# A hybrid decoder layer on one core: block one's softmax ahead of block two's masks, block two's transposes over four PSUM banks, the keys' transposes after both rotations

## The chip, the core and the metric

The kernel runs on one core of a Trainium2 chip. The metric is the device time of one execution in microseconds; lower is better. TensorE (PE) multiplies matrices, VectorE (DVE) and ScalarE (ACT) do the elementwise work, and SyncE (SP) issues the loads of the weights.

## The reference

One decoder layer over 256 tokens (two blocks of 128) of width 2048, in float32. Cut to what matters here:

```
h = rmsnorm(x); proj = h @ w_in
xr, yr, q, k, v, g_rnn, g_attn = split(proj)
xr = rg_lru(causal_conv(xr));  y_rnn = xr * gelu(yr)
q, k = rope(q), rope(k)                       # 32 query heads, 4 key/value heads of 64
scores = q k^T * 64**-0.5, masked: at most 127 tokens back, causal
m = max(max(scores), sink); p = exp(scores - m)
probs = p / (sum(p) + exp(sink - m));  y_att = probs @ v
mix = sigmoid(g_rnn) * (y_rnn @ w_rnn_proj) + sigmoid(g_attn) * (y_att @ w_attn_proj)
x = x + rmsnorm(mix @ w_out)
x = x + rmsnorm(relu(rmsnorm(x) @ w_mlp_up)**2 @ w_mlp_down)
```

## The kernel before

Every weight is streamed once from HBM in halves of 128 x 1024 float32. ScalarE rounds a half to its high part (`whi`, L94), VectorE subtracts to get the low part (`wlo`, L95), and TensorE makes three products of high and low parts for each tile. The `Stream` object splits about six halves ahead of their use, in six buffers for each part, and loads into four more (`wraw`).

The stages follow one another: keys and values; then for each of four groups of heads (one key/value head and eight query heads, `g` = 0 to 3) a pass over the attention's gates (`g`, 96 matmuls with 512 columns, two accumulators in one pair of PSUM banks, ended by `tanh` on ScalarE, L647) and a pass over the queries (`q`, 96 matmuls); then the recurrence's projections (`recur`, in calls of `a_pair`), the projections of the mixers, the output projection, and the MLP.

The work that belongs to no weight pass is written as generators in a list `waiting`. A pass calls `pump()` at fixed places, which runs the first generator to its next `yield`. `keys_values` runs in the first gates' pass. `attention(g)` begins after the queries' pass of group g and so runs in the next group's two passes, and for the last group in the four `a_pair` calls of `recur(0)`. A scheduler orders each engine's instructions from there; those that `pin` marks keep their order. Each engine then works through its own list strictly in order, and waits where a semaphore is not there yet.

`first_norm` (L434) gets the rows' norms, scales the rotation's tables, and spreads the norm over the partitions by two matmuls (`pr`, L448), copied by ScalarE to `rT` (L449), which `conv` and `gelu` use much later. `keys_values` (L515) rotates a block's keys, has them transposed by TensorE (`pk`, L526) and copied to `kT` (L527), and then does the second block.

In `attention` (L532), the queries are rotated and transposed (`pq`). `scores(tb, j, banks)` multiplies them with the keys (`sc`, L560), and VectorE scales and masks the scores (L566) and takes their maximum (L568). `softmax(tb)` makes the small statistics on VectorE (L575 to L577), the exponentials with their sums on ScalarE (L582), and normalises on VectorE (L584, L585, L587). `turn_probs(tb)` transposes the probabilities on TensorE (`pt`, L604), eight transposes for block one and sixteen for block two, four to a bank, and ScalarE copies each bank (L606). The output matmuls (`po`, L630) follow. Block one sees 128 keys, block two 256, so block two's scores take twice as many passes.

PSUM has eight banks: the pool `psa` with two pairs of banks (`pair`, `two_banks`), and here `psb` and `psm` with two single banks each. A tile that is allocated takes the pool's buffers in turn and waits until the former tile in it has been read.

Before the MLP, the second block's normalised rows are transposed (`turned(1, q)`, `ptr`, L921) as soon as VectorE has them (L915). While TensorE would wait, it does steps of the first MLP projection for block one (`up_step(0, j, k)`, L977), 44 ahead of and between the four transposes, and four behind them:

```
todo = [(j, k) for j in (0, 2, 1, 3, 4, 5) for k in range(8)]
for q, n in enumerate((26, 6, 6, 6)):
    for j, k in todo[:n]:
        pin(up_step(0, j, k))
```

## Time and profile before

| | |
|---|---|
| median of 3 runs | 1517.41 us (1516.36 to 1518.62) |
| profiled execution | 1517.5 us, its span 1515.7 us |
| granted TensorE clock | 0.998 |
| busy: TensorE, VectorE, ScalarE | 1493.5, 1102.2, 829.2 us |
| HBM | 195 GB/s over the span |

Times in the timelines count from the span's start. A row gives the start, the time to the end of the last instruction in it, the engine, the line, the operation, what it writes and reads, how many instructions were merged, and in brackets the idle time of the engine before and what ended it. A matmul's length overlaps the next one's, so steps are read from start to start. In lists of waits a row gives the total in us, the number of waits, and the longest.

### The profile page before, as it was taken

How to read it: one execution, taken by the hardware profiler on the slowest of the kernel's cores; microseconds unless marked ns; L12 is line 12 of the kernel's file. 1: busy time of each engine (PE TensorE's matmuls, PEld its weight loads, DVE VectorE, ACT ScalarE, POOL GpSimd, SP SyncE). 2: the span in 40 equal slices, each digit the busy share in tenths (PEclk: the TensorE clock that was granted, in tenths of full speed). 3: DMA queues.
4: the chain of work that ended last, by engine and by line, in shares of the span. 5: the costliest groups of instructions: out<-in, count | busy, mean ns of one | idle time of the engine just before them, and what ended most of it. 6: DMA issues, size and time to landing. Idle time of an engine off the chain costs nothing.

```text
span 1515.7 us, 20016 instructions
## 1 busy us (share of the span) xinstructions
PE 1493.5 (99%) x7600; PEld 1259.8 (83%) x7600; DVE 1102.2 (73%) x1377; ACT 829.2 (55%) x1143; POOL 5.5 (0%) x11
## 2 busy tenths in 40 slices
PE   9999999999999999999999999999999999999996
PEld 7787778788888888888888888888888888888875
DVE  6666677858769966555667866798886666688897
ACT  6554654646566766443355655555454455555543
POOL 0000000000000000000000000000000000000001
PEclk9999999999999999999999999999999999999999
DMA  6645445465646565655764756566657555566564
GB/s 253 218 144 187 142 131 170 153 196 166 217 159 215 174 209 196 191 183 194 268 225 137 271 183 193 185 203 213 219 195 239 194 188 188 193 236 213 195 209 174
DMA packets 82895, 296.19 MB, mean 195 GB/s; under 512 B 9712, under 2 KB 9968, under 8 KB 81648
## 3 DMA queue, kind: packets, MB, share of 16 engines
q1 hardware_dynamic: 79056, 284.43, 57.4%
q10 hardware_dynamic: 3744, 10.50, 1.9%
q8 instruction: 59, 0.97, 0.2%
q14 instruction: 36, 0.29, 0.1%
HBM read 288.60 MB, written 6.29 MB: 195 GB/s over the span
## 4 chain that ended last, share of the span: by engine, by line
PE 82%; DVE 9%; DMA 4%; ACT 2%; issue 2%; DVEq 0%; SPq 0%; ACTq 0%
PE ps L256 21%; PE ps L254 11%; PE dQ L1084 4%; DMA wraw<-in_w_dn 4%; PE pp L294 4%; PE pp L296 4%; PE pp L298 4%; PE g L294 3%; DVE wlo L95 3%; PE g L298 3%; PE g L296 3%; PE s L1084 3%; PE dP L1084 2%; PE q L296 2%; PE q L298 2%; PE q L294 2%
## 5 line engine op out<-in xcount | busy, mean ns | idle before, releaser
L94 ACT CAST whi<-wraw 128x1024 fp32r<-128x1024 f32 x523 | 544.6, 1053 | 567.5 <-PE ps L256 123.7
L95 DVE TENSOR_TENSOR wlo<-wraw,whi 128x1024 fp32r<-128x1024 f32 x523 | 632.8, 1221 | 301.9 <-ACT whi L94 295.2
L256 PE MATMUL ps<-h2T,whi 128*128 128x512 f32 x960 | 223.9, 390 | 0.0
L256 PEld LDWEIGHTS ps<-h2T,whi 128*128 128x128 f32 x960 | 178.2, 188 | 35.6
L256 PE MATMUL ps<-hT,whi 128*128 128x512 f32 x512 | 121.3, 391 | 0.0
L254 PEld LDWEIGHTS ps<-h2T,wlo 128*128 128x128 f32 x960 | 119.1, 192 | 2.3
L254 PE MATMUL ps<-h2T,wlo 128*128 128x256 f32 x960 | 119.9, 283 | 0.0
L256 PEld LDWEIGHTS ps<-hT,whi 128*128 128x128 f32 x512 | 94.7, 188 | 20.1 <-issue 1.5
L1084 PE MATMUL dQ<-whi,uT 128*128 128x512 f32 x288 | 106.9, 389 | 0.0
L294 PE MATMUL g<-whi,hT 128*128 128x512 f32 x256 | 101.2, 395 | 0.0
L296 PE MATMUL g<-wlo,hT 128*128 128x512 f32 x256 | 100.0, 391 | 0.1
L298 PE MATMUL g<-whi,hT 128*128 128x512 f32 x256 | 99.8, 390 | 0.0
L254 PE MATMUL ps<-hT,wlo 128*128 128x256 f32 x512 | 64.9, 283 | 0.0
L254 PEld LDWEIGHTS ps<-hT,wlo 128*128 128x128 f32 x512 | 63.8, 191 | 1.2
L1084 PEld LDWEIGHTS dQ<-whi,uT 128*128 128x128 f32 x288 | 54.1, 188 | 11.2
L1084 PE MATMUL dQ<-wlo,uT 128*128 128x512 f32 x144 | 56.4, 391 | 1.2 <-DVE wlo L95 1.1
L294 PEld LDWEIGHTS g<-whi,hT 128*128 128x128 f32 x256 | 48.1, 188 | 10.6 <-issue 1.0
L298 PEld LDWEIGHTS g<-whi,hT 128*128 128x128 f32 x256 | 48.1, 188 | 10.2
L296 PEld LDWEIGHTS g<-wlo,hT 128*128 128x128 f32 x256 | 48.1, 188 | 9.9 <-DVE wlo L95 0.5
L1084 PE MATMUL dCs<-whi,uT 128*128 128x512 f32 x144 | 54.1, 389 | 0.0
L1084 PE MATMUL dP<-whi,uT 128*128 128x512 f32 x144 | 54.1, 389 | 0.0
L130 DVE TENSOR_TENSOR tlo<-t,thi 128x1536 fp32r<-128x1536 f32 x28 | 49.2, 1756 | 5.5 <-ACT thi L129 5.3
(280 smaller groups left out, 2462.1 us busy)
## 6 DMA issues: line engine op xcount, KB each, us to landing
wraw<-in_w_up SPq DMA_DIRECT2D x128, 512.0 KB, 4.1
wraw<-in_w_dn SPq DMA_DIRECT2D x128, 512.0 KB, 4.8
wraw<-in_w_g SPq DMA_DIRECT2D x64, 512.0 KB, 4.7
wraw<-in_w_xy SPq DMA_DIRECT2D x64, 512.0 KB, 4.5
wraw<-in_w_q SPq DMA_DIRECT2D x32, 512.0 KB, 4.4
wraw<-in_w_ap SPq DMA_DIRECT2D x32, 512.0 KB, 4.6
wraw<-in_w_rp SPq DMA_DIRECT2D x32, 512.0 KB, 4.1
wraw<-in_w_out SPq DMA_DIRECT2D x32, 512.0 KB, 4.9
```

The lines of the kernel that those rows point to most:

```text
L94: self.pin(self.nc.scalar.copy(hi, src))
L95: self.pin(self.nc.vector.tensor_tensor(lo, src, hi.bitcast(F32), ALU.subtract))
L130: v.tensor_tensor(lo, t, hi.bitcast(F32), ALU.subtract)
L254: mm(ps[:, f, 1, :], w, a[:, 0, :], start=False, stop=j == 1 and k == 7)
L256: mm(ps[:, f].rearrange("p a b -> p (a b)"), w, a.rearrange("p a b -> p (a b)"), start=kt == 0, stop=j == 3 and k == 7)
L294: mm(banks[tb][n], a[:, 0, t], hi[:, n * 512 : n * 512 + 512], start=first, stop=False)
L296: mm(banks[tb][n], a[:, 0, t], lo[:, n * 512 : n * 512 + 512], start=False, stop=False)
L298: mm(banks[tb][n], a[:, 1, t], hi[:, n * 512 : n * 512 + 512], start=False, stop=last)
L1084: mm(b, a[x], w[y], start=not begun and i == 0, stop=tail and i == 2)
```

## The change

- `first_norm` no longer issues the two spreading matmuls and the copy to `rT`. A new function `spread_out` does, and is called after the keys' transposes.
- `keys_values` rotates both blocks' keys first, and transposes both in one step, with extra `yield`s between.
- In `attention`, `softmax(0)` is called ahead of `scores(1, ...)`, instead of behind it. One more `yield` stands behind `softmax(1)`.
- For groups 0 to 2, block two's sixteen transposes use a pair of banks of `psa` beside the two of `psm`. For the last group they are called in two halves, and the steps are further apart.
- Before the MLP, 30 instead of 26 steps stand ahead of the second block's first transposes.

The number of instructions on every engine stays the same. In the order as built, block one's transposes of probabilities move up by 19 (group 0) or 13 matmuls (groups 1 and 2), and back by ten in group 3; block two's sixteen stand together behind 24 matmuls of the queries' pass (in groups 1 and 2 with one matmul between the twelfth and the thirteenth); the outputs (`po`) stand 23 or 24 matmuls behind them. The second block's keys' transposes still stand ten matmuls behind the first's.

```
     def first_norm():
-        pr = bank(psm, "pr")
-        spread = t2("spread")
         for tb in range(TB):
             ...
-            mm(pr[:, tb * P : tb * P + P], ones, dg, start=True, stop=True)
-        nc.scalar.copy(rT, pr[:, 0:S])
+    def spread_out():
+        pr = bank(psm, "pr")
+        for tb in range(TB):
+            mm(pr[:, tb * P : tb * P + P], ones, spread[:, tb * P : tb * P + P], start=True, stop=True)
+        nc.scalar.copy(rT, pr[:, 0:S])

     def keys_values(banks):
         yield
         first_norm()
+        keys = []
         for tb in range(TB):
             ...
             rope(banks[tb][:, 0:256], tb, NKV, [k4[:, :, 0, :], k4[:, :, 1, :]])
             yield
+        yield
+        yield
+        for tb in range(TB):
             ps = bank(psm, "pk")
             for g in range(NKV):
-                nc.tensor.transpose(ps[:, g * P : g * P + P], k2[:, g * P : g * P + P], ident)
+                nc.tensor.transpose(ps[:, g * P : g * P + P], keys[tb][:, g * P : g * P + P], ident)
             nc.scalar.copy(kT[:, :, tb * P : tb * P + P], ps.rearrange("p (g t) -> p g t", g=NKV))
-            yield
+        yield
+        spread_out()
+        yield

-        def turn_probs(tb):
+        def turn_probs(tb, pars=(0, 1), banks=()):
             ...
-            for par in range(2):
+            for par in pars:
                 for kb in range(nk):
-                    ps = bank(psm, "pt")
+                    ps = banks.pop(0) if banks else bank(psm, "pt")

         scores(0, 0, [bank(psm, "sc") for par in range(2)])
+        softmax(0)
         scores(1, 0, [bank(psb, "sc") for par in range(2)])
         if not last_group:
             scores(1, 1, two_banks("sc"))
-        softmax(0)
         yield
         if last_group:
             scores(1, 1, [bank(psb, "sc") for par in range(2)])
         softmax(1)
         yield
-        turn_probs(0)
         yield
-        yield
-        turn_probs(1)
-        yield
+        if last_group:
+            yield
+            turn_probs(0)
+            yield
+            yield
+            yield
+            turn_probs(1, (0,))
+            yield
+            turn_probs(1, (1,))
+            yield
+            yield
+        else:
+            turn_probs(0)
+            yield
+            yield
+            turn_probs(1, banks=two_banks("pt"))
+            yield

-    for q, n in enumerate((26, 6, 6, 6)):
+    for q, n in enumerate((30, 6, 6, 6)):
```

More of the change, by code (lines that the diff above doesn't have):

```diff
@@ L432, in layer @@
     rT = pa.tile([P, S], F32, name="rT")
+    spread = t2("spread")
     def first_norm():
-        pr = bank(psm, "pr")
-        spread = t2("spread")
         for tb in range(TB):
@@ L445, in first_norm @@
                 nc.vector.tensor_scalar(t[:, tb], t[:, tb], r, None, ALU.mult)
-            dg = spread[:, tb * P : tb * P + P]
-            nc.vector.tensor_scalar(dg, ident, r, None, ALU.mult)
-            mm(pr[:, tb * P : tb * P + P], ones, dg, start=True, stop=True)
+            nc.vector.tensor_scalar(spread[:, tb * P : tb * P + P], ident, r, None, ALU.mult)
+    def spread_out():
+        pr = bank(psm, "pr")
+        for tb in range(TB):
+            mm(pr[:, tb * P : tb * P + P], ones, spread[:, tb * P : tb * P + P], start=True, stop=True)
         nc.scalar.copy(rT, pr[:, 0:S])
@@ L517, in keys_values @@
         first_norm()
+        keys = []
         for tb in range(TB):
             nc.scalar.activation(v_sb[:, tb, :], banks[tb][:, 256:512], AF.Copy, scale=r0[tb])
-            k2 = t2("k2")
-            k4 = k2.rearrange("p (g c d) -> p g c d", g=NKV, c=2)
+            keys.append(t2("k2"))
+            k4 = keys[tb].rearrange("p (g c d) -> p g c d", g=NKV, c=2)
             rope(banks[tb][:, 0:256], tb, NKV, [k4[:, :, 0, :], k4[:, :, 1, :]])
             yield
+        yield
+        yield
+        for tb in range(TB):
             ps = bank(psm, "pk")
             for g in range(NKV):
-                nc.tensor.transpose(ps[:, g * P : g * P + P], k2[:, g * P : g * P + P], ident)
+                nc.tensor.transpose(ps[:, g * P : g * P + P], keys[tb][:, g * P : g * P + P], ident)
             nc.scalar.copy(kT[:, :, tb * P : tb * P + P], ps.rearrange("p (g t) -> p g t", g=NKV))
-            yield
+        yield
+        spread_out()
+        yield
     yatt = []
@@ L590, in attention @@
         pT = {}
-        def turn_probs(tb):
+        def turn_probs(tb, pars=(0, 1), banks=()):
             nk = 1 + tb
             per = 4 // nk
-            if tb:
-                room_p = flat(unit("pT", F32)).rearrange("p (n c) -> p n c", c=512)
-            else:
-                room_p = rooms[tb][:, 2:4, :]
-            for par in range(2):
+            if pars[0] == 0:
+                rooms["p", tb] = (flat(unit("pT", F32)).rearrange("p (n c) -> p n c", c=512) if tb
+                                  else rooms[tb][:, 2:4, :])
+            room_p = rooms["p", tb]
+            banks = list(banks)
+            for par in pars:
                 for kb in range(nk):
-                    ps = bank(psm, "pt")
+                    ps = banks.pop(0) if banks else bank(psm, "pt")
                     for h in range(4):
```

## The prediction

> **What bounds the kernel now.** I read the page's head first, then the list of waits for TensorE alone, then the timelines of the attention stage engine by engine.

> ```profile
> span 1515.7 us, 20016 instructions
> PE 1493.5 (99%) x7600; PEld 1259.8 (83%) x7600; DVE 1102.2 (73%) x1377; ACT 829.2 (55%) x1143; POOL 5.5 (0%) x11
> ```
> ```profile
> PE pt L604 <- DVE s L587: 4.4, 3, 1.5
> ...
> PE pr L448 <- DVE spread L447: 0.9, 1, 0.9
> PE ptr L921 <- DVE h L915: 0.7, 1, 0.7
> ```

> TensorE sets the end: it is busy for 1493.5 of 1515.7 us. No edit takes matmul work away, so the change can only win back time in which TensorE stands. The three rows are the stalls at the places it touches: transposes of probabilities (pt), the spread of the first norm (pr), block two's transposes before the MLP (ptr), together 6.0 us.

> The first stall is typical in group 1, start and length in us:

> ```profile
> 154.62 0.39 PE L298 MATMUL g<-whi,hT 128*128 128x512 f32 x1
> ...
> 160.97 0.39 PE L294 MATMUL q<-whi,hT 128*128 128x512 f32 x1
> 162.78 1.23 PE L604 MATMUL pt<-ident,s 128*128 128x128 f32 x8 [1.42 <-DVE s L587]
> ...
> 169.36 1.03 PE L604 MATMUL pt<-ident,s 128*128 128x128 f32 x8
> ```
> ```profile
> 149.42 1.28 DVE L566 SCALAR_TENSOR_TENSOR s<-sc,mask 128x512 f32<-128x512 f32 x2
> ...
> 156.57 0.15 DVE L575 TENSOR_TENSOR stat<-stat,sink 128x8 f32<-128x8 f32 x1
> ...
> 161.50 0.17 DVE L584 TENSOR_TENSOR stat<-stat 128x8 f32<-128x8 f32 x1 [1.94 <-ACT s L582]
> ...
> 161.94 1.29 DVE L587 TENSOR_TENSOR s<-s,stat 128x512 f32<-128x512 f32 x2
> ```
> ```profile
> 158.29 0.39 ACT L582 ACTIVATE s<-s,stat 128x128 f32<-128x128 f32 x1
> ...
> 161.47 0.49 ACT L582 ACTIVATE s<-s,stat 128x256 f32<-128x256 f32 x1
> ...
> 165.41 1.05 ACT L606 COPY s<-pt 128x512 f32<-128x512 f32 x2
> ...
> 167.31 1.26 ACT L647 ACTIVATE m<-g,st 128x512 f32<-128x512 f32 x2
> ```

> A projection matmul starts every 0.227 us (28 steps from 154.62 to 160.97). The transposes were due at 161.20 and began at 162.78: the normalising pass starts at 161.94, and its first tile is used 0.84 us after that. The eight then take 0.20 longer than the unhindered eight at 169.36 (0.11 each), waiting for the second tile. DVE did twelve mask and maximum passes for both blocks (7.15 us, 0.596 each) before block one's statistics; only then could ScalarE begin block one's eight exponentials (3.18 us).

> **Groups 1 and 2.** The built order of the changed kernel puts block one's three small statistics between block two's masks, 0.08 us each, and L584 right behind the last maximum: 156.57 + 0.24 = 156.81. The exponentials now start behind the sixth pass, at 153.2, and end at 156.6, so DVE, not ScalarE, is late by a little. L587 follows L584 by 0.44, at 157.25, so block one's first transposes can start at 158.09, and the second bank's at 158.70. They also stand 13 matmuls earlier on TensorE: 161.20 - 13 x 0.227 = 158.25, second bank 158.69. So the stall of 1.58 goes, and the 0.20: 1.8 us for this group, and 1.8 for group 2, which holds another of the three stalls in the list and runs the same instructions. The match at the second bank is to 0.01 us: there is no reserve, and each tenth DVE is late is lost in each group.

> Block two's sixteen transposes stand together, 24 matmuls into the next pass, over two free banks and two of the pair that the gates' pass has left. TensorE gets there at 158.25 + 0.88 (eight transposes) + 36 x 0.227 = 167.3. The pair is free behind the tanh (L647). ScalarE's new queue up to there, from 156.6: a cast 0.95, eight wide exponentials 4.0, a cast, two copies 0.94, a cast, two tanh 1.26: about 165.7. That is covered by 1.6 us. Two casts and the low-part subtractions behind them come 4 to 6 us later than now. A half of the weights feeds twelve matmuls, 2.7 us, and about five halves lie split ahead of the next cast, 13 us of work, so I cost that at nothing; without that cover each microsecond would be a stall. A late subtraction also holds back a load by as much; that reaches ScalarE's later casts, ahead of the copies of pt, and the outputs (po) have moved 24 matmuls behind the transposes, 5.4 us, which covers it.

> **Group 0.**

> ```profile
> 95.69 1.28 DVE L566 SCALAR_TENSOR_TENSOR s<-sc,mask 128x512 f32<-128x512 f32 x2
> ...
> 104.12 0.16 DVE L575 TENSOR_TENSOR stat<-stat,sink 128x8 f32<-128x8 f32 x1
> ...
> 104.61 1.22 DVE L95 TENSOR_TENSOR wlo<-wraw,whi 128x1024 fp32r<-128x1024 f32 x1
> ```
> ```profile
> 108.15 0.39 PE L296 MATMUL q<-wlo,hT 128*128 128x512 f32 x1
> ...
> 109.06 1.23 PE L604 MATMUL pt<-ident,s 128*128 128x128 f32 x8
> ```

> Here the transposes move 19 matmuls up (due three steps after 108.15, at 108.83, now; at 104.52 then), and the built order leaves block two's three statistics ahead of L584; in a chain they take 0.49 (104.12 to 104.61). L584 at 95.69 + 7.15 + 0.24 + 0.49 = 103.57, L587 104.01, first bank 104.85, second 105.46: waits of 0.33 and 0.17. Today 0.23 is lost at the start and 0.20 at the second tile. The term is 0.

> **Group 3**, beside the recurrence's first matmuls:

> ```profile
> 268.38 1.32 PE L256 MATMUL ps<-hT,whi 128*128 128x512 f32 x5
> 271.25 0.63 PE L604 MATMUL pt<-ident,s 128*128 128x128 f32 x4 [1.54 <-DVE s L587]
> ...
> 278.31 2.19 PE L254 MATMUL ps<-hT,wlo 128*128 128x256 f32 x17
> 280.60 0.63 PE L604 MATMUL pt<-ident,s 128*128 128x128 f32 x4
> ```
> ```profile
> 274.56 0.16 DVE L576 TENSOR_SCALAR stat<-stat 128x8 f32<-128x8 f32 x1
> ...
> 279.33 0.17 DVE L584 TENSOR_TENSOR stat<-stat 128x8 f32<-128x8 f32 x1 [2.07 <-ACT s L582]
> ```
> ```profile
> 275.14 0.51 ACT L582 ACTIVATE s<-s,stat 128x256 f32<-128x256 f32 x1
> ```

> Block one's transposes were due at 269.5 and began at 271.25; with the smaller waits behind (0.25 at 280.60, more at the banks) the group loses 2.3 us. In the new order they stand ten matmuls later, at 271.8, and their data by DVE's rows at 270.1 and 270.7: no wait. But DVE now has one more low-part subtraction (1.13 us) ahead of block two's L576: 275.7 instead of 274.56. ScalarE, which began block two's exponentials at 275.14, begins at 275.9; L584 moves from 279.33 to 280.1, the first normalised tile can be used at 281.4, the third at 282.6. TensorE reaches block two's transposes at 271.8 + 0.88 + 17 x 0.227 + 32 x 0.12 = 280.4. It waits 1.0, does three, and waits 0.9 more. So 1.9 comes back and 0.4 is left; between 0 and 2.3 if DVE is later or earlier.

> **Keys and spread.**

> ```profile
> 45.10 0.49 PE L448 MATMUL pr<-spread,ones 128*128 128x128 f32 x2 [0.85 <-DVE spread L447]
> ...
> 54.57 0.66 PE L526 MATMUL pk<-ident,k 128*128 128x128 f32 x4
> ```
> ```profile
> 47.18 0.37 ACT L449 COPY rT<-pr 128x256 f32<-128x256 f32 x1
> 47.97 1.05 ACT L94 CAST whi<-wraw 128x1024 fp32r<-128x1024 f32 x1 [0.42 <-ACT rT L449]
> 49.04 1.28 ACT L486 ACT_TABLE_LOAD   x1
> ```
> ```profile
> 49.06 1.23 DVE L95 TENSOR_TENSOR wlo<-wraw,whi 128x1024 fp32r<-128x1024 f32 x1 [0.15 <-ACT whi L94]
> 50.63 0.30 DVE L494 TENSOR_SCALAR ss<-turns 128x64 f32<-128x64 f32 x2 [0.35 <-ACT turns L486]
> ```

> The spread costs 1.66 us ahead of the keys' transposes: a stall of 1.0 (0.85 shown idle, the rest under the modelled end of the matmul before) and four passes in two places, 0.65. Without them TensorE is there at 52.9. The name says one burst; the built order keeps ten matmuls between the two groups of four, where they stood. But the rotated keys were only just ready at 54.57. Their chain gains 0.7: without rT's copy the cast at 47.97 starts at 47.18, the table load ends at 49.5 and leaves the path, DVE's L95 starts 0.3 earlier, and L494, 1.13 behind it, at 49.9 instead of 50.63. So pk starts at 53.9: 0.95 of new wait. The spread is then paid beside the second transposes, 0.44. Net 1.66 - 0.95 - 0.44 = 0.3, between 0 and 1.2.

> **Before the MLP.**

> ```profile
> 813.80 1.60 PE L977 MATMUL ps<-h2T,whi 128*128 128x256 f32 x12
> 816.13 0.66 PE L921 MATMUL ptr<-ident,h 128*128 128x128 f32 x4 [0.74 <-DVE h L915]
> ```

> Four more steps of 0.12 us fill 0.5 of the stall; they are taken from behind the last transposes, where the next twelve steps need only the first quarter's copies. Gain 0.5, bound 0.

> **Sum:** 0.3 + 0 + 1.8 + 1.8 + 0.4 + 0.5 = 4.8 us. The profiled execution took 1517.5 us (span 1515.7), beside a median of 1517.41; 1517.5 - 4.8 = 1512.7. Everything after is led by TensorE, so the gain stays.

> [...]

> ```profile
> 1.08 4.63 PE L366 MATMUL warm<-ones 128*128 128x128 f32 x20 [1.08 <-DVE ones L350]
> ```

> At the start a 128-wide pass takes 0.21 us, for some 5 us; later eight transposes take 0.88, 0.11 each, and matmuls right behind keep 0.23. [...]

> **Rivals.** *All stalls vanish* (chance 0.08): keys 1.2, group 0 0.5, groups 1 and 2 3.6, group 3 2.3, ptr 0.5: 8.1, 1509.4 us. It needs DVE about a microsecond faster in its order, which no row supports. *The stall only moves* (0.14): the transposes stand 13 matmuls earlier, so a DVE chain later by 1 us in groups 1 and 2 takes 2 us back, and a full loss in group 3 leaves about 2: 1515.5, within 0.2%. *Slower* (0.04): the four banks wait for tanh. If ScalarE's casts ahead of it wait for a load,

> ```profile
> ACT whi L94 <- DMA wraw<-in_w_dn: 26.3, 18, 5.0
> ```

> as long as the longest 5.0 us elsewhere, three groups lose 5.0 - 1.6 each: 10.2 - 4.8 = 5.4 us, 1522.9. It turns the sign from 3.2 us of lateness; no cast waits for a load in this stage now. *Slower by the clock* (0.02): if each of three bursts set half rate for the 5 us of the start, 3 x 2.5 = 7.5 us, 1520.2. [...] *Forecast*: 0.72.

> **Numbers.** 0.2%, about what a measurement can tell here, is 3.0 us: 1514.4. The range runs from 1510.3 (keys and group 3 better by 2.4) to 1515.6 (groups 1 to 3 worse by 2.9), leaving out both slower cases and part of the first two rivals. Faster 0.78 (0.70 of the forecast and the first rival), within 0.2% 0.16, slower 0.06.

> **What would show it.** In the changed profile: pt's wait on s near 0 in groups 1 and 2, half a microsecond in group 0, two waits of nearly 1 us at block two's transposes in group 3; pr without a wait, and a new one of 0.9 at pk on k; ptr's wait near 0.25. It is wrong if pt waits on m (the tanh) or on the copies, if po waits on pT, or if a projection waits on wlo between 95 and 290 us.

## The result and the profile after

The changed kernel took 1520.44 us (median of 20 runs, 1516.73 to 1523.02), the kernel before beside it 1515.17 us (20 runs, 1513.26 to 1518.62). The ratio is 1.0032 (95% interval 1.0025 to 1.0039): about 4.9 us slower, where 4.8 us faster was forecast. The profiled execution took 1519.08 us.

The head of the changed kernel's page, and its list of waits for TensorE:

```profile
span 1517.3 us, 20020 instructions
PE 1493.6 (98%) x7600; PEld 1262.6 (83%) x7600; DVE 1101.2 (73%) x1377; ACT 829.1 (55%) x1143; POOL 5.5 (0%) x11
```
```profile
PE pt L613 <- ACT pT L615: 6.5, 3, 2.4
PE ptr L375 <- DMA x<-in_x: 1.9, 1, 1.9
PE pt L613 <- DVE s L595: 1.7, 3, 0.8
...
PE pk L532 <- DVE k L511: 0.8, 1, 0.8
PE dQ L1106 <- DVE wlo L95: 0.4, 1, 0.4
PE ptr L943 <- DVE h L937: 0.2, 1, 0.2
```

(Lines have moved: the exponentials are L590, the normalising L595, the probabilities' transposes L613, their copies L615.) Most rows are as forecast or nearly: `pt` waits for normalised data for 1.7 us instead of 4.4, `pr` is gone, `pk` waits 0.8, `ptr` of the MLP (L943) 0.2. The first row is new: the transposes wait three times, once in each of groups 0 to 2, for ScalarE's copy of transposes. Group 1 in the timelines of TensorE, ScalarE, VectorE and SyncE's queue:

```profile
160.47 1.04 PE L613 MATMUL pt<-ident,s 128*128 128x128 f32 x8
161.26 0.48 PE L294 MATMUL g<-whi,hT 128*128 128x512 f32 x1
...
169.54 1.47 PE L613 MATMUL pt<-ident,s 128*128 128x128 f32 x12
170.77 0.48 PE L294 MATMUL q<-whi,hT 128*128 128x512 f32 x1
173.69 0.66 PE L613 MATMUL pt<-ident,s 128*128 128x128 f32 x4 [2.45 <-ACT pT L615]
```
```profile
167.66 2.00 ACT L94 CAST whi<-wraw 128x1024 fp32r<-128x1024 f32 x2
172.11 1.04 ACT L94 CAST whi<-wraw 128x1024 fp32r<-128x1024 f32 x1 [2.45 <-DMA wraw<-in_w_q]
173.06 2.04 ACT L615 COPY pT<-pt 128x512 f32<-128x512 f32 x4
```
```profile
160.72 1.22 DVE L95 TENSOR_TENSOR wlo<-wraw,whi 128x1024 fp32r<-128x1024 f32 x1
...
164.24 2.50 DVE L595 TENSOR_TENSOR s<-s,stat 128x512 f32<-128x512 f32 x4
166.65 4.63 DVE L95 TENSOR_TENSOR wlo<-wraw,whi 128x1024 fp32r<-128x1024 f32 x4
```
```profile
167.90 0.33 SPq L76 DMA_DIRECT2D wraw<-in_w_q  x1
```

Block one's eight transposes at 160.47 wait for nothing: that part came true. Of block two's sixteen, twelve run at 169.54 and four stand until 173.69. What they wait for is the first of the four copies at 173.06; it ends some 0.58 later, at 173.64. It is the copy of the pair's first bank, and the four are those that write the pair's second. The copies stand in ScalarE's queue behind a cast, and that cast stands 2.45 us for a weight load. The load was issued at 167.90, right behind the first of the low-part subtractions at 166.65 (1.13 us from start to start), which frees its buffer.

The rest of the loss is the clock. In the table by stretches (length; busy time and count of each engine; then the granted clock, the share of the DMA engines, GB/s), the third stretch begins 1.4 us behind that wait:

```profile
core 0: us, PE busy (x) PEld busy (x) DVE busy (x) ACT busy (x) POOL busy (x), PEclk, DMA share, GB/s
169.00:172.00 3.00, 2.25 (x17) 1.76 (x15) 2.28 (x3) 0.67 (x1) 0.00 (x0) 1.00 0.70 238
172.00:175.00 3.00, 1.30 (x8) 1.19 (x9) 1.23 (x1) 2.89 (x5) 0.00 (x0) 1.00 0.88 284
175.06:178.47 3.41, 3.41 (x9) 2.65 (x9) 0.00 (x0) 0.15 (x2) 0.00 (x0) 0.50 0.73 293
178.50:182.00 3.50, 3.50 (x16) 2.22 (x16) 1.23 (x1) 1.65 (x2) 0.00 (x0) 1.00 0.04 6
```

For 3.41 us the clock is 0.50: eight matmuls start in that time, 0.43 us apart instead of 0.227, so about 1.6 us are lost.

How much each stage takes is read from TensorE's timeline, from the first matmul of one stage to the first of the next. The differences from the kernel before, in us, with two kernels of the experiments below:

| stage | forecast | after | issue order changed | steps apart |
|---|---|---|---|---|
| up to the first gates' pass | 0 | +0.24 | -0.40 | -0.59 |
| to group 0's scores (keys, spread) | -0.3 | -0.29 | +0.43 | -1.27 |
| group 0 | 0 | +2.26 | +0.11 | -0.52 |
| group 1 | -1.8 | +2.50 | -1.81 | -1.84 |
| group 2 | -1.8 | +0.57 | -1.83 | -1.83 |
| group 3 | -0.4 | -0.34 | -0.35 | -2.16 |
| from there to the last stage (`dQ`), with `ptr` | -0.5 | -0.44 | -0.44 | -0.47 |
| sum | -4.8 | +4.50 | -4.29 | -8.68 |

Behind that the profiled execution of before loses 2.9 us more than that of after, so that the two spans differ by only 1.6 us. No edit acts there, and the twelve profiles of this study lie up to 3.3 us apart in that stretch. The runs taken together show the 4.9.

### The profile page after: what moved, and what is told of

It is laid out like the page before. It is cut to its first block, busy times and chain, and to the rows that moved or that the text cites. A ratio compares the mean times of both kernels' runs of the same rounds, so it can differ in the third digit from the quotient of the medians.

```text
span 1517.3 us, 20020 instructions
## 1 busy us (share of the span) xinstructions
PE 1493.6 (98%) x7600; PEld 1262.6 (83%) x7600; DVE 1101.2 (73%) x1377; ACT 829.1 (55%) x1143; POOL 5.5 (0%) x11
## 4 chain that ended last, share of the span: by engine, by line
PE 89%; DVE 5%; DMA 2%; ACT 2%; issue 1%; DVEq 0%; SPq 0%; ACTq 0%
PE ps L256 21%; PE ps L254 11%; PE dQ L1106 8%; PE s L1106 5%; PE dP L1106 4%; PE pp L298 4%; PE pp L296 4%; PE pp L294 4%; PE g L294 3%; PE g L298 3%; PE g L296 3%; PE dCs L1106 3%; PE o L294 2%; PE o L296 2%; PE o L298 2%; PE q L294 2%
## 5 line engine op out<-in xcount | busy, mean ns | idle before, releaser
L95 DVE TENSOR_TENSOR wlo<-wraw,whi 128x1024 fp32r<-128x1024 f32 x523 | 632.1, 1221 | 311.5 <-ACT whi L94 306.0
L94 ACT CAST whi<-wraw 128x1024 fp32r<-128x1024 f32 x523 | 544.4, 1053 | 557.4 <-PE ps L256 129.3
L256 PE MATMUL ps<-h2T,whi 128*128 128x512 f32 x960 | 223.9, 390 | 0.0
L256 PEld LDWEIGHTS ps<-h2T,whi 128*128 128x128 f32 x960 | 178.2, 188 | 35.7
L254 PEld LDWEIGHTS ps<-h2T,wlo 128*128 128x128 f32 x960 | 119.1, 192 | 2.3
L256 PE MATMUL ps<-hT,whi 128*128 128x512 f32 x512 | 121.1, 391 | 0.0
L254 PE MATMUL ps<-h2T,wlo 128*128 128x256 f32 x960 | 119.9, 283 | 0.0
L256 PEld LDWEIGHTS ps<-hT,whi 128*128 128x128 f32 x512 | 94.6, 188 | 19.3 <-issue 0.7
L294 PE MATMUL g<-whi,hT 128*128 128x512 f32 x256 | 101.4, 396 | 0.0
L296 PE MATMUL g<-wlo,hT 128*128 128x512 f32 x256 | 100.0, 390 | 0.1
L298 PE MATMUL g<-whi,hT 128*128 128x512 f32 x256 | 99.8, 390 | 0.0
L254 PEld LDWEIGHTS ps<-hT,wlo 128*128 128x128 f32 x512 | 63.7, 191 | 2.0 <-issue 0.8
L254 PE MATMUL ps<-hT,wlo 128*128 128x256 f32 x512 | 64.4, 283 | 0.0
L294 PEld LDWEIGHTS g<-whi,hT 128*128 128x128 f32 x256 | 48.1, 188 | 10.4 <-issue 1.0
L298 PEld LDWEIGHTS g<-whi,hT 128*128 128x128 f32 x256 | 48.0, 188 | 10.2
L296 PEld LDWEIGHTS g<-wlo,hT 128*128 128x128 f32 x256 | 48.1, 188 | 10.0 <-DVE wlo L95 0.5
```

Source lines behind the costliest of these rows:

```text
L94: self.pin(self.nc.scalar.copy(hi, src))
L95: self.pin(self.nc.vector.tensor_tensor(lo, src, hi.bitcast(F32), ALU.subtract))
L254: mm(ps[:, f, 1, :], w, a[:, 0, :], start=False, stop=j == 1 and k == 7)
L256: mm(ps[:, f].rearrange("p a b -> p (a b)"), w, a.rearrange("p a b -> p (a b)"), start=kt == 0, stop=j == 3 and k == 7)
L294: mm(banks[tb][n], a[:, 0, t], hi[:, n * 512 : n * 512 + 512], start=first, stop=False)
L296: mm(banks[tb][n], a[:, 0, t], lo[:, n * 512 : n * 512 + 512], start=False, stop=False)
```

## The experiments

All ratios are to the kernel before, with 95% intervals.

**The order of issue.** The theory: the late copy is needed only because the loop issues the pair's second four transposes behind the copy of its first four, and the pair is one tile.

```
             for par in pars:
+                turned_to = []
                 for kb in range(nk):
                     ...
                         nc.tensor.transpose(...)
+                    turned_to.append(ps)
+                for kb, ps in enumerate(turned_to):
                     t = room_p[:, par * nk + kb, :]
                     nc.scalar.copy(t, ps)
```

> Only the order of issue in turn_probs is changed: block two's transposes of a pair of banks are issued in one run, and the two copies behind them, so that the pair's second bank no longer waits for the copy of its first. Theory (the late copy): the wait of the transposes for ScalarE's copy in groups 0 to 2, 7.2 us in the profile after (2.1 + 2.7 + 2.4), goes, with it the half-rate window behind group 1's (about 1.6 us), and the kernel comes to what the prediction's steps gave without it: ratio to the kernel before 0.995 to 0.998 (1508 to 1512 us). Rival (the sixteen transposes in one burst lower the clock by themselves, whoever waits): half-rate windows stay, and the ratio stays at 1.000 or above. Rival (the copy still stands behind the held-up casts, so the next user of the banks waits in place of the transposes): 1.001 to 1.003, with a wait for the pT copies at po's matmuls or at the gates' next pass.

Measured: 1511.2 us against 1514.97, ratio 0.9973 (0.9964 to 0.9982). TensorE's and ScalarE's timelines in group 1:

```profile
167.48 1.91 PE L614 MATMUL pt<-ident,s 128*128 128x128 f32 x16
169.15 0.48 PE L294 MATMUL q<-whi,hT 128*128 128x512 f32 x1
```
```profile
169.75 1.05 ACT L94 CAST whi<-wraw 128x1024 fp32r<-128x1024 f32 x1 [2.16 <-DMA wraw<-in_w_q]
170.71 2.04 ACT L618 COPY pT<-pt 128x512 f32<-128x512 f32 x4
```

The cast still stands 2.16 us for its load and the copies are about as late as they were (23.5 us behind the group's first scores, 23.8 in the changed kernel), but nobody waits for them: the sixteen run in one, the outputs come 24 matmuls later, and the clock stays at 1.00 from 7 us to the end of TensorE's work (0.998 in the mean of the span, 0.995 in the profile after). Each term of the table returns to the forecast, but for the keys: here TensorE was 0.6 us earlier at the start than in the profile after, and waited about as much longer for them.

**The small banks.** Block two's transposes over the two banks of `psm`, one tile to a bank:

```
-            turn_probs(1, banks=two_banks("pt"))
+            turn_probs(1)
```

> The changed kernel, but block two's transposes of groups 0 to 2 go over the two banks of the small pool, one tile to a bank, as before the change (8, then 8), not over the pair behind the gates' pass. Theory (the late copy): block two's second eight need a copy of a bank that block one or block two left, again by ScalarE, behind the same casts; a wait of 0.5 to 2.5 us in each of three groups, ratio 0.999 to 1.003. Rival (the pair is what costs, by its one tile for two banks): these waits are gone, ratio 0.995 to 0.998.

Measured: 1520.12 us against 1514.97, ratio 1.0033 (1.0023 to 1.0042), just above what the theory had given. Its list of waits:

```profile
PE pt L613 <- ACT pT L615: 6.2, 3, 2.2
```

So giving up the pair does not help. With a tile to each bank, block two's later transposes need a bank to be copied out as well, and the copy is about as late (the longest wait is 2.2 us, 2.4 in the changed kernel). In both kernels the burst that reuses a bank, or is made to look so, took over the lateness of ScalarE's queue: 6.2 us here, 6.5 there.

**The softmax alone.** The kernel before, with `softmax(0)` ahead of `scores(1, ...)` and nothing else.

```
         scores(0, 0, [bank(psm, "sc") for par in range(2)])
+        softmax(0)
         ...
-        softmax(0)
         yield
```

> The kernel before with one edit: the softmax of block one stands ahead of the scores of block two. Theory (the late copy): the prediction's gain at block one's transposes shows (1.8 us in each of groups 1 and 2), the held-back weights are split later behind the softmax, so some of it comes back as waits for them or for the copies; ratio 0.997 to 1.001. Rival (moving the softmax alone makes the casts late, and the pair has no part in it): 1.001 to 1.004.

Measured: 1519.44 us against 1514.97, ratio 1.0033 (1.002 to 1.0045). I had expected part of the gain to show, and that was wrong; the ratio lies in the rival's range, but the list of waits names another wait than the rival's, and none for the copies.

```profile
PE pt L604 <- DVE s L587: 6.8, 4, 1.9
```

The wait is for block one's normalising, as before, and is longer than the 4.4 us there: without the further step behind `softmax(1)` the transposes are placed still earlier in the gates' pass, before their data. Moved alone, the softmax gains nothing. That it needs the step is read from the built order (in groups 1 and 2 the transposes stand 26 matmuls of the gates' pass behind the scores, 36 in the changed kernel); no run adds the step alone. The third of these waits, 1.92 us, was followed by 3.4 us at half rate (a matmul every 0.43 us).

**The softmax back.** The changed kernel, with `softmax(0)` behind all of block two's masks, where it was; the pair and the steps stay.

```
         scores(0, 0, [bank(psm, "sc") for par in range(2)])
-        softmax(0)
         scores(1, 0, [bank(psb, "sc") for par in range(2)])
         if not last_group:
             scores(1, 1, two_banks("sc"))
+        softmax(0)
```

> The changed kernel, but the softmax of block one stands behind all of block two's masks again; the pair, the steps and the keys' burst stay. Theory (the late copy: the softmax ahead delays the low parts, these hold back the next weight load, ScalarE's cast stands for it and block two's copies behind that): the wait of the transposes for the copies, 6.5 us in the profile after, falls below 2 us, and the wait for block one's normalising (4 to 5 us in the kernel before) is back; ratio to the kernel before 0.998 to 1.001. Rival (one tile for the pair's two banks makes the wait whatever the softmax does): both waits stand, 6 us and 4 us, and the ratio is 1.003 to 1.007.

Measured: 1513.3 us against 1515.03, ratio 0.9989 (0.9981 to 0.9997). Group 1 in VectorE's, SyncE's and ScalarE's timelines:

```profile
156.28 1.21 DVE L95 TENSOR_TENSOR wlo<-wraw,whi 128x1024 fp32r<-128x1024 f32 x1
...
157.98 1.22 DVE L95 TENSOR_TENSOR wlo<-wraw,whi 128x1024 fp32r<-128x1024 f32 x1
```
```profile
157.52 2.03 SPq L76 DMA_DIRECT2D wraw<-in_w_q  x2
```
```profile
168.08 2.00 ACT L94 CAST whi<-wraw 128x1024 fp32r<-128x1024 f32 x2
169.97 2.03 ACT L615 COPY pT<-pt 128x512 f32<-128x512 f32 x4
```
```profile
PE pt L613 <- DVE s L595: 3.6, 3, 1.4
```

Here both low parts are done before the exponentials, at 156.28 and 157.98; the two loads go out from 157.52 on; no cast waits; the copies come at 169.97 and the wait for them is gone from the list, although pair and issue order are the changed kernel's. Block one's stall is back. In the changed kernel the second of these subtractions starts at 166.65 and its load at 167.90. That is 8.7 us later on the clock of the timelines, but the group's scores begin 2.6 us later there too, so the delay within the group is 6.1 us. This delay is what the cast waits for. The run changes the order in ScalarE's queue as well: the cast that stands in the changed kernel comes behind the copies here (at 171.88), and three matmuls instead of one stand between the twelfth and the thirteenth transpose. So it shows that the lateness comes with the softmax, but not how much of the wait each of these makes.

**The copies on VectorE.** The changed kernel, with block two's copies of groups 0 to 2 taken out of ScalarE's queue:

```
-                    nc.scalar.copy(t, ps)
+                    if tb and not last_group:
+                        nc.vector.tensor_copy(t, ps)
+                    else:
+                        nc.scalar.copy(t, ps)
```

> The changed kernel, but in groups 0 to 2 block two's four copies run on VectorE instead of ScalarE. In its queue they stand behind four low-part subtractions, whose weights are all loaded by then, and ahead of the fifth. Theory (ScalarE's queue, with a cast that stands for a load ahead of the copies, makes the wait): the transposes wait less than 1.2 us in each of the three groups instead of 2.1 to 2.7, and the ratio is 0.996 to 0.9995. Rival (the second bank's wait for the first bank's copy costs the same on any engine): the wait stays above 1.9 us in each group, ratio 1.002 or above.

Measured: 1513.75 us against 1515.03, ratio 0.9991 (0.9982 to 0.9999).

```profile
PE pt L613 <- DVE pT L616: 2.2, 3, 0.9
```
```profile
169.91 1.05 ACT L94 CAST whi<-wraw 128x1024 fp32r<-128x1024 f32 x1 [2.19 <-DMA wraw<-in_w_q]
```

The wait falls from 6.5 to 2.2 us (0.4, 0.9 and 0.9), with pair and order of issue as in the changed kernel, and with the cast of group 1 still standing 2.19 us for its load. What made the wait long was that the copies stood behind that cast in ScalarE's queue.

**The keys alone.** The kernel before, with only the keys' burst and the later spread, the first two functions of the change's diff:

```
         for tb in range(TB):
             ...
             yield
+        yield
+        yield
+        for tb in range(TB):
             ps = bank(psm, "pk")
             ...
-            yield
+        yield
+        spread_out()
+        yield
```

> The kernel before with one edit: the keys' transposes in one burst after two more steps, and the spread of the scale after them. By the prediction's terms this is worth 0.3 us less; with its new wait at the first of the keys' transposes 0.9 us are given back there. Ratio 0.999 to 1.001. Rival (the loss is made at the start, by the burst and by a lower clock there): 1.002 to 1.004.

Measured: 1515.46 us against 1514.97, ratio 1.0002 (0.9993 to 1.001); this part cannot be told from no change, and the loss is not made here.

**A long burst of transposes.** The kernel of the changed issue order, with each of block two's transposes issued three times:

```
-                    for h in range(4):
+                    for h in list(range(4)) * (3 if tb and not last_group else 1):
```

> The kernel of the changed issue order, with each of block two's transposes in groups 0 to 2 issued three times over, the same result each time: 48 in one run instead of 16, 96 more in all. By 0.109 us each they cost 10.5 us, which makes about 1521.7 us, ratio 1.004 to 1.0055. Theory (TensorE's idle time, not its transposes, lowers the clock): full rate behind each run of 48 and no more than 11 us added. Rival (a run of transposes counts as idle): half-rate windows like those behind the waits, 1.5 us of loss each, within or behind each run, and more inside the run, so 15 us or more added: 1526 us or above, ratio 1.0075 or more. [...]

Measured: 1521.23 us against 1515.03, ratio 1.0041 (1.0028 to 1.0054), 10 us above the kernel with sixteen; 96 transposes at the 0.108 us each that the rows below show make 10.4. Group 1, and the stretch around it:

```profile
170.54 5.40 PE L614 MATMUL pt<-ident,s 128*128 128x128 f32 x48
175.70 0.47 PE L294 MATMUL q<-whi,hT 128*128 128x512 f32 x1
```
```profile
166.00:176.00 10.00, 10.00 (x70) 9.14 (x69) 7.51 (x8) 7.20 (x12) 0.00 (x0) 1.00 0.54 173
```

And in group 0, where the 48 run from 113.85 to 119.01, one whole interval between two points of the 3.413 us grid that the last section measures, and the next one:

```profile
114.44:117.85 3.41, 3.41 (x34) 3.41 (x32) 1.59 (x2) 1.06 (x1) 0.00 (x0) 1.00 0.82 281
117.85:121.26 3.41, 3.41 (x23) 3.05 (x22) 1.50 (x2) 2.58 (x5) 0.00 (x0) 1.00 0.89 345
```

48 transposes take 5.16 us to the next matmul, 0.108 each, at a granted clock of 1.00. The interval that holds nothing but transposes is followed by 1.00 too. A run of 48 transposes did not lower the clock here.

**A wait made on purpose.** The changed issue order, with one tile of block two's probabilities multiplied by 1.0 four, four and five times before its transposes.

```
+            if tb:
+                for again in range((4, 4, 5, 0)[g]):
+                    nc.vector.tensor_scalar(tiles[1][0][0], tiles[1][0][0], 1.0, None, ALU.mult)
```

> The changed issue order, with a wait made on purpose ahead of block two's transposes in groups 0 to 2: one of its tiles of probabilities is multiplied by 1.0 four, four and five times over on VectorE, between the low-part subtractions that follow. By the times in the profile of the changed issue order the transposes are due some 4 us behind the normalising, and the tile is ready 6.1, 6.0 and 7.8 us behind it: TensorE stands about 2.5, 3 and 4.8 us. Question: what does a wait of TensorE cost beside itself? Theory (a wait of some length lowers the granted clock): each of the three is followed by a half-rate window of 3.4 us, as the 2.45 us of group 1 in the profile after was, 1.5 us of loss each, 4 to 5 us beside the waits of 10 us; ratio 1.005 to 1.009. Rival (the one window after was chance and has nothing to do with the wait): no window, 10 us, ratio 1.002 to 1.005.

Measured: 1520.21 us (10 runs, 1515.89 to 1523.47) against 1515.87, ratio 1.0025 (1.0013 to 1.0037). The waits came out at 1.12, 1.92 and 2.21 us, shorter than planned, since a repeated pass took 0.42 us and I had put in 0.6. Group 1, and the stretches behind the second and third wait and around the first:

```profile
171.42 3.22 PE L617 MATMUL pt<-ident,s 128*128 128x128 f32 x16 [1.92 <-DVE s L599]
```
```profile
171.90:175.30 3.40, 3.40 (x17) 3.21 (x16) 1.73 (x2) 3.13 (x5) 0.00 (x0) 0.50 0.82 242
229.90:233.30 3.40, 3.40 (x13) 3.01 (x14) 1.23 (x1) 2.08 (x5) 0.00 (x0) 0.50 0.81 252
112.00:120.00 8.00, 6.88 (x39) 5.70 (x38) 6.56 (x8) 5.37 (x9) 0.00 (x0) 1.00 0.57 182
```

The two long waits (1.92 and 2.21 us) are each followed by 0.50, the short one (1.12 us) is not: the stretch around it shows 1.00. With 48 transposes in one run at 1.00, the lower clock goes with the wait here and not with the transposes, and not with every wait. The ratio itself fell in the range of the rival, since the waits add up to 5.3 us instead of 10; it is the half rate in the profile that decides between the two.

**Fewer waits.** From the changed issue order on, the waits that were left got a step more: the keys' transposes, block one's of group 0, block two's of group 3.

```
     # keys_values
         yield
         yield
+        yield
         for tb in range(TB):
             ps = bank(psm, "pk")
             ...
-        yield
         spread_out()
         yield
     # attention, last group
             yield
             yield
             yield
+            yield
             turn_probs(1, (0,))
             yield
             turn_probs(1, (1,))
             yield
-            yield
     # attention, other groups
+            if g == 0:
+                yield
             turn_probs(0)
             yield
-            yield
+            if g:
+                yield
             turn_probs(1, banks=two_banks("pt"))
```

> The kernel of the changed issue order, with its four other waits given more room: the keys' transposes one step later (the spread right behind them), block one's transposes of group 0 one step later, block two's of group 3 one step later. In the profile of the changed issue order these waits cost 1.6 (keys), 0.4 (group 0) and 1.8 us (group 3). Theory (each is a wait for work that is ready within one step): up to 3.8 us less than that kernel, ratio to the kernel before 0.9945 to 0.9965. Rival (the waits move to the next user, po or the next keys' work, or the loads): the ratio stays at 0.997 to 0.998.

Measured: 1509.43 us against 1515.03, ratio 0.9961 (0.9949 to 0.9973). Two waits moved on rather than went:

```profile
PE po L658 <- ACT pT L618: 1.3, 1, 1.3
...
PE pk L533 <- DVE k L511: 1.0, 1, 1.0
```

The second block's keys had not moved with the first's, and group 3's outputs now came too early. So both got their step, the outputs of group 3 by the `yield` that had been taken away, the keys like this (against the changed kernel):

```
         yield
         yield
         for tb in range(TB):
+            yield
             ps = bank(psm, "pk")
             ...
-        yield
         spread_out()
-        yield
```

> The changed issue order with the waits of the run before given room once more: the two blocks' key transposes each a step later and one step apart (the spread right behind the second), block one's transposes of group 0 a step later, block two's of group 3 a step later, and now the outputs of group 3 a step later too, since they took over 1.4 us of the wait there. Theory (each wait is for work that is ready within one step): the waits of the keys (1.2 us) and of the outputs (1.4 us) in the profile of the run before go too, 1 to 2.6 us less than it: ratio to the kernel before 0.9935 to 0.9955. Rival (the waits move on again): 0.996 as in the run before.

Measured: 1507.54 us (5 runs, 1506.61 to 1508.9) against 1515.87, ratio 0.9943 (0.9931 to 0.9956), the fastest kernel of this study, 0.57% ahead of the one before. No wait of `pt`, `pk` or `po` is left in its list.

## Why the prediction was wrong

*The terms that were forecast are right, but for the keys, which stay open.* Group 3 -0.34 (forecast -0.4) and `ptr` -0.44 (-0.5) stand in the profile after as they are; groups 1 and 2 show -1.81 and -1.83 (-1.8 each) as soon as the new wait is taken away; group 0 +0.11 (0). The waits forecast for group 3 (1.0 and 0.9) came as 0.93 and 0.85, counted from start to start. The keys' -0.29 (-0.3) and the wait of `pk`, 0.93 (0.95), match as well, but that is partly luck: over the eight profiles with the same edit of the keys the term lies between -0.39 and +0.43, and the idle time before `pk` between 0.65 and 1.47 us.

*The step that failed* is "Block two's sixteen transposes stand together ... over two free banks and two of the pair". I took four banks as four free places. But the pair is one tile, and the loop issues its first bank's transposes, the copy of that bank, then its second bank's transposes: so the last four wait for the copy. That adds 2.1, 2.7 and 2.4 us to groups 0, 1 and 2, 7.2 us in all (counted from start to start; the list shows the 6.5 us of it beyond the modelled end of the matmul before). The lateness itself was forecast: the subtractions were to come "4 to 6 us later", and the second came 6.1 us later within the group. The prediction had the two halves of it in hand, that the lateness of the subtractions comes to "ScalarE's later casts, ahead of the copies of pt", and that the outputs are covered by 24 matmuls. The changed issue order shows that the cover of the outputs is real. What was missing was the other reader of those copies, the burst itself. The built order showed it: in groups 1 and 2 a single matmul between the twelfth transpose and the thirteenth, which needed a reason, and was passed over.

*A second step* was the price of a wait. Group 1's wait of 2.45 us was followed by 3.41 us at 0.50, which cost 1.6 us. The forecast gave such a loss a chance of 0.02 and hung it on the burst, at 2.5 us each. No run shows that term: 48 transposes in one run took 0.108 us each at 1.00. In the run with the made wait, 0.50 followed the waits of 1.92 and 2.21 us.

*The rivals.* "The four banks wait for tanh" if "ScalarE's casts ahead of it wait for a load" had the right late engine and the right cause, a cast that stands for a load, with 1522.9 us, but the wrong place: the first twelve transposes found their banks free. Its bound, "no cast waits for a load in this stage now", was read rightly off the kernel before, but there the subtractions had not moved yet.

*The sum.* -4.8 forecast, +7.2 of waits, +1.6 of clock, and 0.2 at the start, before any edit acts, make +4.2; the profile has +4.5 and the runs +4.9. The 0.2 at the start goes with the clock: in five of the twelve profiles TensorE runs at half rate around 8 to 11 us, behind an interval with 1.88 to 2.12 us of idle time, and these five reach the first gates' pass 0.24 to 0.49 us later than the profile before; the six others reach it 0.25 to 0.6 us earlier. What is left may be the clock as well, whose mean lies between 0.994 and 0.998 in the twelve profiled executions; this was not settled further. The base was also high: the profiled 1517.5 us stood above the later median of 1515.17.

## What to carry to other kernels

Moving work ahead of a queue's other work moved those others' releases back (here a subtraction by 6.1 us within the group); follow the late buffer to its load, to the cast that waits for it, and to everything queued behind that cast, then ask for each of these who reads it, the moved burst included. Two halves of one tile were not two free places (6.5 us of waits here, none for these copies with the issue order changed): issue all writers of a tile before its first reader, or give each half its own tile and make sure that none is reused within the burst. And when a wait goes, look at once for the next one in the list: here an order of issue and a few steps turned a loss of 0.3% into a gain of 0.6%.

## What the runs showed of the hardware

```profile
226.26:229.67 3.41, 2.52 (x18) 2.00 (x16) 2.56 (x3) 1.25 (x2) 0.00 (x0) 1.00 0.71 233
229.67:233.08 3.41, 2.14 (x12) 1.84 (x13) 1.22 (x1) 2.68 (x5) 0.00 (x0) 1.00 0.93 328
233.08:236.50 3.42, 3.42 (x17) 2.79 (x15) 1.22 (x1) 1.05 (x1) 0.00 (x0) 1.00 0.55 212
```
